# A hybrid attention and SSM block: 42 quads with seven products instead of 38, their sums and last blocks in other buffers, the scan's matmuls in program order

## The chip, the cores and the metric

The kernel runs on one core of a Trainium2 chip. The core has a matrix engine (TensorE, PE in the profile), a vector engine (VectorE, DVE), a scalar engine (ScalarE, ACT), a general engine (GpSimd, POOL) and a sync engine (SyncE, SP) that issues DMA transfers; each works through its own list of instructions in order and waits for the others by semaphores. The metric is the device time of one execution in microseconds (us), the median of several runs. Inputs and results are fp32.

## The reference, cut to what matters

One block on 256 rows of 2048: a norm, one wide projection, attention in three dilations with 16 heads, an SSM (convolution, a chunked scan in 8 groups), two gates, and an output projection. The shapes of the weights are 2048 columns wide per q, k, v, z_a, g_a, g_s, 4096 for z_s and xs, 1024 for B and C each.

```python
def hybrid_layer(x, ...):
    hn = rms_norm(x, norm_w)
    proj = hn @ w_in
    q, k, v, z_a, z_s, xbc, dt_raw, g_a, g_s = jnp.split(proj, split_points, axis=-1)
    ...
    outs, lses = ...            # dilated_window_attention for (128, 1), (512, 4), (2048, 16)
    wts = jax.nn.softmax(jnp.stack(lses), axis=0)
    o_a = jnp.einsum('pbsh,pbshe->bshe', wts, jnp.stack(outs)) * jax.nn.silu(z_a)
    xbc = jax.nn.silu(causal_depthwise_conv(xbc, conv_w, conv_b))
    xs, bm, cm = jnp.split(xbc, ...)
    y = ssd_chunked_scan(xs, dt, a, bm, cm) + d_skip * xs
    y = rms_norm(y * jax.nn.silu(z_s), ssm_norm_w)
    merged = jax.nn.sigmoid(g_a) * (o_a @ w_attn_branch) + jax.nn.sigmoid(g_s) * (y @ w_ssm_branch)
    return x + merged @ w_out   # a last rms_norm follows
```

## The kernel before

**Weights.** All weights lie in one array of units, 128 rows by 1024 columns of fp32 (512 KB). Each unit is split in two parts of a reduced format: ScalarE makes the high part h (line 265), VectorE the rest l = w - h (line 266). The left side is split likewise, and a product is the sum of three matmuls, xh.h, xh.l and xl.h (`triple`). Units come through a ring of five places in SBUF (`ring`, tag "w"), the parts through rings of four (h, l, and hl for the seven-product quads). SP issues all of these loads in one queue.

**Stages.** First come the projections that have the weights as columns (z_s, xs, B, C with the SSM's groups 1 to 7, stage by stage), then six pair stages made by `gemm_pair`: ssm (y @ w_ssm_branch, depth 4096, 16 quads), v, later ga, attn (o_a @ w_attn_branch) and out (8 quads each). Between v and ga lie the projections of q, k and z_a and the attention itself. Each pair stage runs in two halves, c = 0 and c = 2, of 1024 columns; "attn half 2" below is the stage ("attn", 2). All 256 rows and 1024 columns stand as 2 x 2 blocks of 128 x 512, four accumulators.

**Quads.** A quad is two units (256 of the depth) times the 2 x 2 blocks: eight products, 24 matmuls of 128x512. For the quads in `S_QUADS` seven products do (Winograd's form of Strassen's scheme): 21 matmuls, for which sums of blocks are needed on both sides. On the weights' side a quad has wa (its first unit), wt (two sums) and the last block, wc, which is half a unit (in the code of before the right half of wb). From them come the split parts ha, la; hc, lc; htt, ltt (of wt) and, after wa -= wt, htu, ltu. The products that are common to several accumulators gather in four more banks (pp) over the stage, and `fold` adds them once at the end.

**Sums made ahead.** Two of the additions for wt can be made ahead (`sum_jobs`): a job loads the blocks into a buffer that stands idle, VectorE subtracts twice (128x512), and the result is spilled to DRAM under the quad's name (t_ssm, t_ga, t_attn, t_out), from where the stage loads it as wt. A copy on POOL ties a job to a place in the program. A quad without such a job loads its second unit whole and makes the two subtractions in place (lines 518 and 524). Of before's 38 quads 30 have their sums ahead: 12 of 13 in ssm, all of ga, attn and out; the seven of v are made in place. Left sums (sx_y for ssm, sx_x, sx_o, sx_m) are also made early and spilled, and fetched when a unit of the stage before is reached (`fetch_left`).

**The scan.** For each of the 8 groups `scan` (line 788) issues 32 matmuls in 16 pairs: the two of a pair write the upper and the lower 64 rows of the result. `after` sets at which unit of the projections the group's scan starts.

**What sets the order.** The code is written stage by stage, but the order on each engine is the scheduler's, by priorities (`high_priority`) and its own estimate of time. It may move a matmul ahead of others that the program wrote before it, where no data forbids it. Rings free a place when the last reader of the old content is done, and a transfer on SP that waits for its place holds those behind it.

Of the kernel before, what the change touches and what calls it, by code (L numbers as in the profile page):

```python
# [15 lines left out]
P = 128  # L16
# [23 lines left out]
A_ORDERS = {0: (0, 1, 2, 4, 3, 6, 5, 7), 2: (0, 2, 1, 4, 3, 6, 5, 7)}  # L40
V_ORDERS = {0: None, 2: (0, 2, 1, 4, 3, 5, 6, 7)}
# [16 lines left out]
SUMS_SSM = [(("ssm", c), q) for c in (0, 2) for q in S_QUADS[("ssm", c)]]  # L58
SSM_EVERY, LEFT_EVERY, ATT_EVERY = 10, 11, 4
SUM_LAG = 3  # L60

# [125 lines left out]
def hybrid_block(ctx: ExitStack, tc: tile.TileContext, wall, xt, x, pk_d, cst_d, fw_d, out):  # L187
    nc = tc.nc
    ve, ac, gp, pe = nc.vector, nc.scalar, nc.gpsimd, nc.tensor

# [221 lines left out]
    def plain_unit(tag, q):  # L412
        return FIRST[tag] + 2 * max(n for n in range(q + 1) if n not in S_QUADS[tag])
# [34 lines left out]
    def gemm_pair(tag, x_of, n_kt, sxs, swap, extra={}, close=1, order=None):  # L448
# [22 lines left out]
        for at, q in enumerate(order):  # L471
# [24 lines left out]
            wa, wb = ring(f"wa{n}"), ring(f"wb{n}")  # L496
# [19 lines left out]
            with tc.high_priority(L_AHEAD):  # L516
# [5 lines left out]
                part(wb[:, 512:], hc[:, :512], lc[:, :512])  # L522
# [131 lines left out]
    with tc.tile_pool(name="ssm", bufs=2) as sp:  # L654
# [125 lines left out]
        def scan(g, state):  # L780
            xdt, gt = state["xdt"], state["gt"]
            yps = [bank("m2", 2, f"yp{g}_{v}") for v in range(2)]
            for k in (3, 2, 1, 0):
                v, i = divmod(k, 2)
                for a, b, c, o in ((0, S, 0, 0), (S, 384, 1, P)):
                    for j in range(2):
                        n, rows, col = 2 * i + j, 64 * j, i * S + o
                        pe.matmul(
                            yps[v][rows : rows + 64, col : col + b - a], xdt[:, v, c, n, :], gt[:, 4 * v + n, a:b],
                            start=(c == 0), stop=(c == 1),  # L790
                        )
# [66 lines left out]
        for c in GS_BEFORE[0]:  # L858
# [6 lines left out]
            SUMS_SSM, range(begin + 1, FIRST[("xs", 26)], SSM_EVERY),  # L865
# [10 lines left out]
        for g in range(GROUPS):  # L876
# [9 lines left out]
            for t in range(max(4 * g, 1), 4 * g + 4):  # L886
# [4 lines left out]
                if t % 4 == 3:  # L891
# [7 lines left out]
                    for q in (2 * g, 2 * g + 1):  # L899
                        if q in SX_Y:  # L900
# [34 lines left out]
    for n, q in enumerate(SX_X[:1]):  # L935
        fetch_left(sx_of_x, xk, 1, ("x", q), two_kts(XT, q), 0, FIRST[("ssm", 2)] + 24 + 4 * n)
    with tc.tile_pool(name="xp", bufs=1) as xp:
        sxs = {}

# [234 lines left out]
```

## Time and profile before

| what | us |
|---|---|
| median of 3 runs | 1389.33 (1388.9 to 1390.08) |
| the profiled execution | 1389.12 |
| its span, first to last instruction | 1387.3 |
| TensorE busy | 1376.8 |
| VectorE busy | 1148.3 |
| ScalarE busy | 828.9 |
| GpSimd busy | 130.3 |
| DMA, mean rate | 240 GB/s |

The profile's numbers are in us, where nothing else is said. "x24" counts instructions. An arrow a<-b names result and operand. An idle time stands with the engine that ended it. In the rows of stretches each engine has its busy time and, in brackets, its instructions; then come the granted clock, the DMA engines' busy share and GB/s. In the rows of the timeline the first number is the start after the span's begin, the second the duration; in the chain's rows the second is the time that the piece adds. Lines of transfers give count, KB each, and the median us from issue to landing.

### The profile page before, as it was taken

Reading aid. Unit: us, or ns where it says so; the run is one execution under the profiler, and the core shown is the slowest. Engines: PE = TensorE matmul, PEld = TensorE weight load, DVE = VectorE, ACT = ScalarE, POOL = GpSimd, SP = SyncE. Lnnn points to the kernel's source line nnn. Section 1 sums busy time; section 2 is a strip of 40 time slices with the busy share of each in tenths; the row PEclk is TensorE's granted clock in tenths of the full one; section 3 lists DMA queues with packets and bytes.
Section 4 is the critical chain, followed back from the end, with each engine's and each line's share of the span. In section 5 each row is a group of like instructions: output and inputs, shape, how many; then the busy total and the mean of one; then the engine's idle time right before and its main releaser. Section 6 shows DMA issues by size and latency. Waiting matters only on the chain.

```text
span 1387.3 us, 20558 instructions
## 1 busy us (share of the span) xinstructions
PE 1376.8 (99%) x7272; PEld 1171.5 (84%) x7272; DVE 1148.3 (83%) x1709; ACT 828.9 (60%) x1289; POOL 130.3 (9%) x201
## 2 busy tenths in 40 slices
PE   9999999999999999999999999999999999999997
PEld 7888888888888888888888888888888888888886
DVE  6898998887798888868878997777777688889897
ACT  7656677675677675765554554544544456556464
POOL 2301110010000000010000001111111000000110
PEclk9999999999999999999999999999999999999999
DMA  9766877868676866567767668888888656776764
GB/s 346 231 189 213 285 241 236 272 200 300 217 251 212 261 197 204 186 228 267 237 224 258 224 195 287 275 274 277 296 287 279 182 171 219 270 250 207 251 241 150
DMA packets 100743, 332.67 MB, mean 240 GB/s; under 512 B 11232, under 2 KB 13472, under 8 KB 100512
## 3 DMA queue, kind: packets, MB, share of 16 engines
q1 hardware_dynamic: 99920, 330.18, 72.0%
q8 instruction: 57, 0.93, 0.3%
q10 hardware_dynamic: 720, 1.18, 0.2%
q14 instruction: 46, 0.38, 0.1%
HBM read 306.87 MB, written 24.44 MB: 239 GB/s over the span
## 4 chain that ended last, share of the span: by engine, by line
PE 98%; DMA 0%; DVE 0%; POOL 0%; SPq 0%; ACT 0%; issue 0%; POOLq 0%; DVEq 0%; ACTq 0%
PE ps_zs L318 8%; PE ps_xs L318 8%; PE ps_zs L321 4%; PE ps_q L318 4%; PE ps_k L318 4%; PE ps_za L318 4%; PE ps_xs L321 4%; PE ps_ssm L463 3%; PE ps_ssm L464 3%; PE ps_ssm L465 3%; PE ps_q L321 2%; PE ps_k L321 2%; PE ps_za L321 2%; PE ps_gs L402 2%; PE ps_gs L403 2%; PE ps_gs L401 2%
## 5 line engine op out<-in xcount | busy, mean ns | idle before, releaser
L265 ACT ACTIVATE h<-w 128x1024 fp32r<-128x1024 f32 (+1 forms) x408 | 425.7, 1049 | 357.2 <-issue 82.8
L266 DVE TENSOR_TENSOR l<-w,h 128x1024 fp32r<-128x1024 f32 (+1 forms) x408 | 491.9, 1211 | 160.9 <-ACT h L265 158.5
L318 PE MATMUL ps_zs<-XT,h 128*128 128x512 f32 x496 | 175.7, 395 | 0.0
L318 PE MATMUL ps_xs<-XT,h 128*128 128x512 f32 x496 | 175.2, 394 | 0.0
L321 PE MATMUL ps_zs<-XT,l 128*128 128x256 f32 x496 | 139.6, 282 | 0.0
L321 PE MATMUL ps_xs<-XT,l 128*128 128x256 f32 x496 | 139.6, 281 | 0.0
L318 PEld LDWEIGHTS ps_xs<-XT,h 128*128 128x128 f32 x496 | 93.0, 188 | 21.3
L318 PEld LDWEIGHTS ps_zs<-XT,h 128*128 128x128 f32 x496 | 93.1, 188 | 20.9
L321 PEld LDWEIGHTS ps_zs<-XT,l 128*128 128x128 f32 x496 | 93.6, 189 | 1.9 <-issue 1.1
L321 PEld LDWEIGHTS ps_xs<-XT,l 128*128 128x128 f32 x496 | 93.6, 189 | 0.8 <-issue 0.6
L318 PE MATMUL ps_q<-XT,h 128*128 128x512 f32 x256 | 92.3, 404 | 0.0
L318 PE MATMUL ps_k<-XT,h 128*128 128x512 f32 x256 | 89.8, 394 | 0.0
L318 PE MATMUL ps_za<-XT,h 128*128 128x512 f32 x256 | 89.5, 394 | 0.0
L321 PE MATMUL ps_q<-XT,l 128*128 128x256 f32 x256 | 71.0, 277 | 0.0
L321 PE MATMUL ps_k<-XT,l 128*128 128x256 f32 x256 | 71.0, 277 | 0.0
L321 PE MATMUL ps_za<-XT,l 128*128 128x256 f32 x256 | 70.9, 277 | 0.0
L318 PEld LDWEIGHTS ps_k<-XT,h 128*128 128x128 f32 x256 | 48.0, 188 | 11.1
L318 PEld LDWEIGHTS ps_za<-XT,h 128*128 128x128 f32 x256 | 48.0, 188 | 11.0
L318 PEld LDWEIGHTS ps_q<-XT,h 128*128 128x128 f32 x256 | 48.0, 188 | 10.9
L751 ACT ACTIVATE gt<-acb,acT 128x128 f32<-128x128 f32 x128 | 43.8, 391 | 19.5 <-DMA acb<-acum_d 16.4
L512 ACT ACTIVATE ha<-wa 128x1024 fp32r<-128x1024 f32 x38 | 40.0, 1054 | 20.8 <-DMA wa<-in_wall 7.4
L513 DVE TENSOR_TENSOR ltu<-wa,htu 128x1024 fp32r<-128x1024 f32 x38 | 46.4, 1222 | 5.8 <-ACT htu L512 5.4
(633 smaller groups left out, 3270.2 us busy)
## 6 DMA issues: line engine op xcount, KB each, us to landing
w<-in_wall SPq DMA_DIRECT2D x404, 512.0 KB, 4.5
wa<-in_wall SPq DMA_DIRECT2D x38, 512.0 KB, 4.4
th_a<-in_wall SPq DMA_DIRECT2D x18, 512.0 KB, 5.5
acb<-acum_d SPq DMA_DIRECT2D x32, 256.0 KB, 3.8
wb<-in_wall SPq DMA_DIRECT2D x30, 256.0 KB, 3.7
sums_at<-in_wall SPq DMA_DIRECT2D x12, 512.0 KB, 4.0
t_ssm<-sums_at SPq DMA_DIRECT2D x12, 512.0 KB, 4.3
wt<-t_ssm SPq DMA_DIRECT2D x12, 512.0 KB, 4.9
```

The lines of the kernel that those rows point to most:

```text
L265: ac.activation(h[:, a:b], w[:, a:b], AF.Copy)
L266: ve.tensor_tensor(l[:, a:b], w[:, a:b], h[:, a:b].bitcast(F32), ALU.subtract)
L318: pe.matmul(acc, h[:, kk, :], m, start=(kt == 0), stop=False)
L321: pe.matmul(acc[:, S:], l[:, kk, :], m[:, :S], start=False, stop=(kt == KT - 1))
L401: pe.matmul(accs[i], xh, h[:, kk], start=(kt == 0), stop=False)
L402: pe.matmul(accs[i], xh, l[:, kk], start=False, stop=False)
L463: pe.matmul(acc, xh, h, start=start, stop=False)
L464: pe.matmul(acc, xh, l, start=False, stop=False)
L465: pe.matmul(acc, xl, h, start=False, stop=stop)
L512: ac.activation(h, src, AF.Copy)
L513: ve.tensor_tensor(l, src, h.bitcast(F32), ALU.subtract)
L751: ac.activation(g4[:, n, b], acb[:, j, b // 2 * P : b // 2 * P + P], AF.Relu, scale=-1.0, bias=sc[:, h : h + 1],)
```

## The change

- `S_QUADS`: seven products for ssm quad 12 in both halves, v quad 5 in half 0 and attn quad 5 in half 2; 42 in all. The orders in which quads come within a half are new for ssm, and changed for v half 0 and attn half 2.
- `SUMS_SSM` now lists ssm and v, except for ssm quad 12 (`IN_PLACE`). The jobs start at three units of each of groups 1 to 6: 18 places for 13 + 8 entries, and the zip ends with the shorter, so v half 2 quads 4, 5 and 6 have no job and are summed in place. Sums ahead: 13 ssm, 5 v, 8 ga, 7 attn, 4 out; in place: 5.
- `place` in `gemm_pair`: a quad with its sum ahead no longer takes ring places for wt and the last block (wc), but seats in a `room`, a buffer that is idle in that stage, round robin: for ssm two seats for wc in the stage's pool, for v all in room_v, for ga wt in th_a's idle half, for attn wt and wc in `fin` (a new name and buffer for the result of attn, where vt was), for out in room_o. In attn the seats of wc are `fin[:, 0, :512]` and `fin[:, 1, :512]`, which are also two of the four blocks that take the result of half 0. The count of seats runs on from one half to the next.
- The left sums of ssm quads 12 and 13 are made in the stage itself (`Y_LATE`), by way of a ring place, and not spilled and fetched.
- `scan` issues its matmuls under `in_order`, so the scheduler keeps them in the order written, with nothing between that comes from elsewhere in the list.

```diff
--- before.py
+++ after.py
-A_ORDERS = {0: (0, 1, 2, 4, 3, 6, 5, 7), 2: (0, 2, 1, 4, 3, 6, 5, 7)}
-V_ORDERS = {0: None, 2: (0, 2, 1, 4, 3, 5, 6, 7)}
+A_ORDERS = {0: (0, 1, 2, 4, 3, 6, 5, 7), 2: (0, 2, 1, 4, 3, 5, 6, 7)}
+V_ORDERS = {0: (0, 1, 2, 4, 3, 5, 6, 7), 2: (0, 2, 1, 4, 3, 5, 6, 7)}
...
 S_QUADS = {
-    ("ssm", 0): (5, 7, 8, 10, 11, 13), ("ssm", 2): (3, 5, 7, 8, 10, 11, 13),
-    ("v", 0): (2, 4, 6), ("v", 2): (2, 4, 5, 6), ("ga", 0): (2, 4, 5, 6), ("ga", 2): (2, 4, 5, 6),
-    ("attn", 0): (2, 4, 6), ("attn", 2): (2, 4, 6), ("out", 0): (3, 5), ("out", 2): (3, 5),
+    ("ssm", 0): (5, 7, 8, 10, 11, 12, 13), ("ssm", 2): (3, 5, 7, 8, 10, 11, 12, 13),
+    ("v", 0): (2, 4, 5, 6), ("v", 2): (2, 4, 5, 6), ("ga", 0): (2, 4, 5, 6), ("ga", 2): (2, 4, 5, 6),
+    ("attn", 0): (2, 4, 6), ("attn", 2): (2, 4, 5, 6), ("out", 0): (3, 5), ("out", 2): (3, 5),
 }
-SX_Y = S_QUADS[("ssm", 2)]
+Y_ORDERS = {0: (0, 1, 2, 3, 5, 4, 7, 8, 6, 10, 11, 9, 12, 14, 13, 15), 2: (0, 3, 1, 5, 2, 7, 8, 4, 10, 11, 6, 12, 9, 13, 14, 15)}
+Y_LATE = {12: 4, 13: 6}
+SX_Y = sorted({*S_QUADS[("ssm", 0)], *S_QUADS[("ssm", 2)]}, key=Y_ORDERS[0].index)
...
-SUMS_SSM = [(("ssm", c), q) for c in (0, 2) for q in S_QUADS[("ssm", c)]]
-SSM_EVERY, LEFT_EVERY, ATT_EVERY = 10, 11, 4
+IN_PLACE = {"ssm": [(0, 12), (2, 12)]}
+SUMS_SSM = [(t, q) for t in (("ssm", 0), ("ssm", 2), ("v", 0), ("v", 2)) for q in S_QUADS[t] if (t[1], q) not in IN_PLACE.get(t[0], ())]
+SUM_UNITS = 2, 9, 16
+LEFT_EVERY, ATT_EVERY = 11, 4
...
+    seats = {}
+
+    def gemm_pair(tag, x_of, n_kt, sxs, swap, extra={}, close=1, order=None, room={}):
...
+            def place(kind):
+                if not room.get(kind):
+                    t = ring(f"{kind}{n}")
+                    return t[:, 512:] if kind == "wc" else t
+                seats[kind] = seats.get(kind, -1) + 1
+                return room[kind][seats[kind] % len(room[kind])]
+
+            wa = ring(f"wa{n}")
             nc.sync.dma_start(wa, wall[n])
             if made:
-                wt = ring(f"wt{n}")
+                wt, wc = place("wt"), place("wc")
                 nc.sync.dma_start(wt, presum[tag, q])
-                nc.sync.dma_start(wb[:, 512:], wall[n + 1, :, 512:])
+                nc.sync.dma_start(wc, wall[n + 1, :, 512:])
             else:
-                wt = wb
-                nc.sync.dma_start(wb, wall[n + 1])
+                wt = ring(f"wb{n}")
+                wc = wt[:, 512:]
+                nc.sync.dma_start(wt, wall[n + 1])
...
-                part(wb[:, 512:], hc[:, :512], lc[:, :512])
+                part(wc, hc[:, :512], lc[:, :512])
...
+                        in_order(
+                            pe.matmul(
+                                yps[v][rows : rows + 64, col : col + b - a], xdt[:, v, c, n, :], gt[:, 4 * v + n, a:b],
+                                start=(c == 0), stop=(c == 1),
+                            )
...
-            SUMS_SSM, range(begin + 1, FIRST[("xs", 26)], SSM_EVERY),
+            SUMS_SSM, [FIRST[("B", g)] + n for g in range(1, 7) for n in SUM_UNITS],
...
+    def room_of(t, n_wt, n_wc):
+        t = t.rearrange("p (n m) -> p n m", m=512)
+        return {
+            "wt": [t[:, 2 * n : 2 * n + 2].rearrange("p n m -> p (n m)") for n in range(n_wt)],
+            "wc": [t[:, 2 * n_wt + n] for n in range(n_wc)],
+        }
+
     with tc.tile_pool(name="xp", bufs=1) as xp:
         sxs = {}
+        ssm_room = room_of(xp.tile([P, ROOM_SSM * 512], F32, name="room_s", tag="room"), 0, ROOM_SSM)
...
+        def left_y(q):
+            spare = Y_SPARE[q]
+            sx = new_sx(xp, sum(s == spare for s in Y_SPARE.values()), spare, f"y{q}")
+            sxs[q] = turn_x(sx, ring(f"sxt_y{q}").rearrange("p (n m) -> p n m", n=2), two_kts(yT, q), spare)
...
-                ("ssm", c), lambda kt: kt_of(yT, kt), 2 * KT, sxs, c == 2, {} if c else {2: [scale_gate]}
+                ("ssm", c), lambda kt: kt_of(yT, kt), 2 * KT, sxs, c == 2, {} if c else {2: [scale_gate], **{u: [lambda q=q: left_y(q)] for q, u in Y_LATE.items()}},
+                1, Y_ORDERS[c], ssm_room,
...
+    room = room_of(big.tile([P, 6 * 512], F32, name="room_v", tag="yo0a"), 2, 2)
...
+        room = {"wt": [th_a[:, i, UNIT:] for i in range(2)]}
...
-        fin = vt
+        fin = big.tile([P, 2, D], F32, name="fin", tag="yo1a")
+        room = {"wt": [fin[:, i, UNIT:] for i in range(2)], "wc": [fin[:, i, :512] for i in range(2)]}
...
-            dst = blocks(vt, c)
+            es, prods = gemm_pair(
+                ("attn", c), lambda kt: kt_of(oaT, kt), KT, sx_of_o, c == 2, order=A_ORDERS[c], room=room
+            )
+            dst = blocks(fin, c)
...
+        out_room = room_of(big.tile([P, 6 * 512], F32, name="room_o", tag="yo1b"), 2, 2)
```

The order before, on TensorE, around group 1's scan (yp; ps_zs and ps_xs are projections, h and l the parts of the weights). One lone matmul of yp stands 24 us ahead of the rest:

```order
L321 MATMUL ps_xs9_2151<-XT_76,l66_2182 128x256
L318 MATMUL ps_zs9_2224<-XT_76,h67_2227 128x512
L788 MATMUL yp1_1_2478<-gt1_1879,xdt1_1946 64x256
L321 MATMUL ps_zs9_2224<-XT_76,l67_2228 128x256
...
L318 MATMUL ps_zs11_2464<-XT_76,h75_2467 128x512
L788 MATMUL yp1_1_2478<-gt1_1879,xdt1_1946 64x256
L788 MATMUL yp1_1_2478<-gt1_1879,xdt1_1946 64x128 x2
...
L788 MATMUL yp1_0_2477<-gt1_1879,xdt1_1946 64x256 x2
```

The same places after:

```order
L324 MATMUL ps_zs9_2237<-XT_76,h67_2240 128x512
L327 MATMUL ps_zs9_2237<-XT_76,l67_2241 128x256
...
L324 MATMUL ps_zs11_2482<-XT_76,h75_2485 128x512
L806 MATMUL yp1_1_2491<-gt1_1888,xdt1_1955 64x256 x2
L806 MATMUL yp1_1_2491<-gt1_1888,xdt1_1955 64x128 x2
...
L806 MATMUL yp1_0_2490<-gt1_1888,xdt1_1955 64x256 x2
```

All 32 stand together at the later place, and so in all eight groups; before, groups 1, 2 and 6 were cut.

SP's queue ahead of attn half 2, whose first seven-product quad has the units 437 and 438, before:

```order
L254 DMA w434_12566<-in_wall 128x1024 [waits DMAHW6_49,DVE_49]
L497 DMA wa437_12600<-in_wall 128x1024 [waits DMAHW7_49,DVE_49]
L500 DMA wt437_12603<-t_attn2_2_10147 128x1024 [waits DMAHW0_49,DVE_49]
L501 DMA wb437_12601<-in_wall 128x512 [waits DMAHW1_49,DVE_49]
L254 DMA w435_12644<-in_wall 128x1024 [waits DMAHW2_49,DVE_49]
```

and after:

```order
L260 DMA w434_12639<-in_wall 128x1024 [waits DMAHW1_49,DVE_49]
L513 DMA wa437_12673<-in_wall 128x1024 [waits DMAHW2_49,DVE_49]
L260 DMA w435_12715<-in_wall 128x1024 [waits DMAHW3_49,DVE_49]
L260 DMA w436_12721<-in_wall 128x1024 [waits DMAHW5_49,DVE_49]
L513 DMA wa441_12751<-in_wall 128x1024 [waits DMAHW7_49,DMAHW4_49,DVE_49]
L260 DMA w439_12793<-in_wall 128x1024 [waits DMAHW0_49,DVE_49]
L517 DMA fin_12264<-in_wall 128x512 [waits DMAHW6_49,DVE_49]
```

The last block of unit 438 went from a ring place right behind wa437 to a seat in `fin`, four weight loads later, where it waits for VectorE.

VectorE there, before (ps_attn0_n are the results of attn half 0; line 1080 adds the folded products, 1071 adds th_a, 1072 makes the merged sum in th_s):

```order
L1080 TENSOR_TENSOR vt_7730<-ps_attn0_3_12192,vt_7730 128x512
L1071 SCALAR_TENSOR_TENSOR th_a_7731<-th_a_7731,vt_7730 128x512
L513 TENSOR_TENSOR la437_12607<-wa437_12600,ha437_12606 128x1024
L1072 SCALAR_TENSOR_TENSOR th_s_90<-th_a_7731,th_s_90 128x512
L513 TENSOR_TENSOR lc437_12611<-wb437_12601,hc437_12610 128x512
...
L266 TENSOR_TENSOR l435_12647<-w435_12644,h435_12646 128x1024
```

and after:

```order
L1125 TENSOR_TENSOR fin_12264<-ps_attn0_3_12268,fin_12264 128x512
L1114 SCALAR_TENSOR_TENSOR th_a_7796<-th_a_7796,fin_12264 128x512
L530 TENSOR_TENSOR la437_12678<-wa437_12673,ha437_12677 128x1024
...
L1115 SCALAR_TENSOR_TENSOR th_s_90<-th_a_7796,th_s_90 128x512
L543 TENSOR_TENSOR wa437_12673<-wa437_12673,fin_12264 128x1024
...
L530 TENSOR_TENSOR lc437_12682<-fin_12264,hc437_12681 128x512
L272 TENSOR_TENSOR l435_12718<-w435_12715,h435_12717 128x1024
```

The parts keep their place among the merges, but lc437 now reads the block from `fin`, whose load waits for the row of line 1114 above; on ScalarE hc437 stands directly ahead of h435, h436 and htu437, as it stood ahead of the former two before.

More of the change, by code (lines that the diff above doesn't have):

```diff
@@ L410, in keep_left, with plain_unit @@
         spill(lefts, key, f"sxd_{key[0]}{key[1]}", sx.bitcast(F32), [2, 4 - spare, P])
-    def plain_unit(tag, q):
-        return FIRST[tag] + 2 * max(n for n in range(q + 1) if n not in S_QUADS[tag])
+    def plain_unit(tag, at, order):
+        return FIRST[tag] + 2 * [q for q in order[: at + 1] if q not in S_QUADS[tag]][-1]
     def new_sx(pool, bufs, spare, name):
@@ L899, in hybrid_block @@
                     for q in (2 * g, 2 * g + 1):
-                        if q in SX_Y:
+                        if q in SX_Y and q not in Y_LATE:
                             after(
@@ L969, in hybrid_block @@
         for c in (0, 2):
-            es, prods = gemm_pair(("v", c), lambda kt: XT[:, kt, :], KT, sx_of_x, c == 2, order=V_ORDERS[c])
+            es, prods = gemm_pair(
+                ("v", c), lambda kt: XT[:, kt, :], KT, sx_of_x, c == 2, order=V_ORDERS[c], room=room
+            )
             dst = blocks(vt, c)
@@ L1051, in hybrid_block @@
             )
+        room = {"wt": [th_a[:, i, UNIT:] for i in range(2)]}
         for c in (0, 2):
-            es, prods = gemm_pair(("ga", c), lambda kt: XT[:, kt, :], KT, sx_of_x, c == 2, order=G_ORDERS[c])
+            es, prods = gemm_pair(
+                ("ga", c), lambda kt: XT[:, kt, :], KT, sx_of_x, c == 2, order=G_ORDERS[c], room=room
+            )
             open_gate(c, es, prods)
@@ L1074, in attend @@
         def attend(c):
-            es, prods = gemm_pair(("attn", c), lambda kt: kt_of(oaT, kt), KT, sx_of_o, c == 2, order=A_ORDERS[c])
-            dst = blocks(vt, c)
+            es, prods = gemm_pair(
+                ("attn", c), lambda kt: kt_of(oaT, kt), KT, sx_of_o, c == 2, order=A_ORDERS[c], room=room
+            )
+            dst = blocks(fin, c)
             with tc.high_priority(M_AHEAD) if c else nullcontext():
```

18 lines of the change are left out of this document (9 added, 9 removed).

## Prediction

> **What bounds the kernel now.** I read the page's engine table first, then its chain, then the list of waits, then equal stretches of time, and only then single places.
>
> ```profile
> PE 1376.8 (99%) x7272; PEld 1171.5 (84%) x7272; DVE 1148.3 (83%) x1709; ACT 828.9 (60%) x1289; POOL 130.3 (9%) x201
> PE 98%; DMA 0%; DVE 0%; POOL 0%; SPq 0%; ACT 0%; issue 0%; POOLq 0%; DVEq 0%; ACTq 0%
> ```
>
> TensorE (PE) is busy for 99% of the span of 1387.3 us and makes up 98% of the chain that ended last. A modelled end can hide small gaps, so the list of TensorE's waits comes next, and after it the stages, one row each: both ssm halves, attn halves 0 and 2, and out half 0.
>
> ```profile
> PE warm L592 <- DVE ssq L589: 1.4, 1, 1.4
> PE ps_first L366 <- ACT h L265: 0.7, 1, 0.7
> ```
>
> ```profile
> 584.70:667.90 83.20, 83.20 (x373) 69.02 (x372) 63.68 (x69) 47.82 (x52) 8.06 (x8) 1.00 0.76 255
> 667.90:750.90 83.00, 83.00 (x368) 68.76 (x367) 66.55 (x66) 45.81 (x49) 2.42 (x2) 1.00 0.70 231
> 1207.60:1249.20 41.60, 41.60 (x186) 34.43 (x185) 36.58 (x41) 25.56 (x30) 0.00 (x0) 1.00 0.70 230
> 1249.20:1292.40 43.20, 43.20 (x200) 35.77 (x199) 41.25 (x53) 23.63 (x30) 1.43 (x1) 1.00 0.70 227
> 1292.40:1336.30 43.90, 43.90 (x203) 36.38 (x202) 37.16 (x47) 22.91 (x29) 7.26 (x4) 1.00 0.76 265
> ```
>
> TensorE waits twice in the whole run, for 2.1 us. In each stage it is full at the granted clock of 1.00, and VectorE (DVE, third busy number) is below it: closest in attn half 2, 41.25 of 43.20. So a matmul that goes is worth its time, as long as VectorE, ScalarE and the loads keep ahead.
>
> **Term 1: four more seven-product quads.** One plain quad is 24 matmuls of 128x512, a seven-product one 21. Attn half 0 holds five and three of them, 183 matmuls in the 41.60 us of its row: 0.227 us each. Single rows agree:
>
> ```profile
> 1248.72 0.39 PE L464 MATMUL ps_attn<-l,oaTb 128*128 128x512 f32 x1
> 1248.95 0.39 PE L465 MATMUL ps_attn<-h,oaTb 128*128 128x512 f32 x1
> 1249.18 0.39 PE L463 MATMUL ps_attn<-h,oaTa 128*128 128x512 f32 x1
> 1249.40 0.39 PE L464 MATMUL ps_attn<-l,oaTa 128*128 128x512 f32 x1
> ```
>
> Starts are 0.227 apart though one lasts 0.39: matmuls overlap, and the pitch counts. 4 x 3 x 0.227 = **-2.72 us**.
>
> Here a page speaks against the reading. The Trainium skill, "Trainium Kernel Development and Optimization", Best Practices, has it that the busy share of matmuls is a poor gauge, since they are pipelined, and that the busy share of weight loads is a good one; the engine table gives 84% for them, which would leave TensorE room, and by 12 loads at the 0.188 us of this profile the term would be an estimated -2.26. The equal starts decide for the pitch.
>
> **Term 2: the scan held together.** The scan's 32 matmuls run as pairs, two halves of 64 columns side by side. The chain shows what a group takes whole and what in pieces (the counts are those on the chain):
>
> ```profile
> 164.51 2.75 PE yp L788 x32
> 202.07 0.58 PE yp L788 x2
> 226.01 2.75 PE yp L788 x23
> 261.03 0.80 PE yp L788 x6
> 287.43 2.31 PE yp L788 x20
> 368.86 2.75 PE yp L788 x32
> 524.34 0.58 PE yp L788 x2
> 550.96 2.75 PE yp L788 x23
> ```
>
> Groups 1 and 6 lose one half of a pair to a place 24 us earlier; the lone half takes 0.58, and the rest still 2.75, since the partner runs alone. Group 2 is cut after three matmuls: 0.80 + 2.31. Against 2.75 the surplus is 0.58 + 0.36 + 0.58 = 1.52. Entering such a place delays the next matmul a little more:
>
> ```profile
> 201.68 0.40 PE L318 MATMUL ps_zs<-XT,h 128*128 128x512 f32 x1
> 202.00 0.65 PE L788 MATMUL yp<-gt,xdt 128*64 128x256 f32 x2
> 202.58 0.39 PE L321 MATMUL ps_zs<-XT,l 128*128 128x256 f32 x1
> ```
>
> Between the two ps_zs lie 0.90 where 0.227 is the pitch: 0.67 lost, 0.09 over the 0.58. With 0.08 to 0.09 for each of the three cuts the term is **-1.77** (ends: -1.52 without it and -1.79). The kept order puts each group whole at the later place, where its operands were already there.
>
> **VectorE, at nothing.** A quad with its sum made ahead costs VectorE four tensor operations of 128x1024 and one of 128x512; a plain quad two of the former; a quad in place two more of 128x512.
>
> ```profile
> 1245.63 1.23 DVE L513 TENSOR_TENSOR ltt<-wt,htt 128x1024 fp32r<-128x1024 f32 x1 [1.48 <-ACT htt L512]
> 1246.77 1.22 DVE L266 TENSOR_TENSOR l<-w,h 128x1024 fp32r<-128x1024 f32 x1
> 1247.91 1.28 DVE L1080 TENSOR_TENSOR vt<-ps_attn,vt 128x512 f32<-128x512 f32 x2
> 1249.10 0.68 DVE L1071 SCALAR_TENSOR_TENSOR th_a<-th_a,vt 128x512 f32<-128x512 f32 x1
> 1249.70 0.69 DVE L1080 TENSOR_TENSOR vt<-ps_attn,vt 128x512 f32<-128x512 f32 x1
> ```
>
> Pitches are 1.14 and 0.60, so 5.16, 2.28 and 6.36. Two of the new quads have their sum ahead (v and attn: 2 x 2.88), two are in place (ssm quad 12 in both halves: 2 x 4.08): +13.9. Five v quads and one ssm quad are no longer in place: 6 x 1.20 = -7.2. Seven more sums made ahead: 7 x 1.20 = +8.4. Some 5 more for the left sums of ssm quad 12, an estimate from operations of these two sizes: +20 on 1148.3, spread over 750 us, against 239 us in which VectorE idles. By stage: ssm half 2 goes from 66.55 by 4.08 - 1.20 to 69.4 of 82.3; attn half 2 with out half 0 gains 2.9 on 78.4 of 87.1. TensorE covers that. If the cover went, each microsecond over would be one of loss; the thin place is attn half 2, taken below.
>
> **Sums ahead, at nothing.** v is not made whole: 13 ssm and 8 v jobs meet 18 places (6 groups by 3), and the last three, of v's second half, stay in place. Seven more jobs bring POOL's copies, two loads and a spill each.
>
> ```profile
> q1 hardware_dynamic: 99920, 330.18, 72.0%
> wt<-t_attn SPq DMA_DIRECT2D x6, 512.0 KB, 4.7
> wb<-in_wall SPq DMA_DIRECT2D x30, 256.0 KB, 3.7
> ```
>
> About 7.5 MB more on 330 at 72% is 1.6 points; POOL stands at 9%. Both lie beside TensorE. A load in a room frees ring places on SP's queue, so weights behind it come no later, except where it waits for the room itself.
>
> **The new wait: start of attn half 2.** Before, the last block of unit 437 lay in the ring long before the stage began (its ring load, 256 KB, takes 3.7), and ScalarE made its high part early:
>
> ```profile
> 1249.66 0.61 ACT L512 ACTIVATE hc<-wb 128x512 fp32r<-128x512 f32 x1
> 1252.11 0.68 DVE L1071 SCALAR_TENSOR_TENSOR th_a<-th_a,vt 128x512 f32<-128x512 f32 x1
> 1252.10 1.07 ACT L265 ACTIVATE h<-w 128x1024 fp32r<-128x1024 f32 x1 [1.82 <-PE ps_attn L465]
> ```
>
> ```profile
> 1257.30 0.66 PE mtp L1064 x6
> ```
>
> Now its seat is the second one in `fin`, which holds block 2 of attn half 0 until VectorE has added it to th_a. Call the stage's first matmul T (1249.18). If VectorE comes as before, that addition is ninth from 1247.91: it ends at 1247.91 + 8 x 0.60 + 0.68 = T+4.2. If only the last matmul of half 0 limits it (1248.95 + 0.39), one eviction and one addition later it ends near T+1.5. The load lands 3.7 later, T+5.2 to T+7.9; hc takes 0.61 (T+5.8 to T+8.5), and behind it in ScalarE's queue stand h435, h436 and htu437, on VectorE lc437, l435, l436: h435 is done near T+6.9 to T+9.6. In the order 27 matmuls and ten transposes (0.11 each) stand ahead of hc437: 27 x 0.227 + 1.1 = T+7.2, and h435 is due a matmul later, T+7.4. The wait is **0 to +2.2**. VectorE's 1.48 us of idling at 1244 says that it isn't far behind there; I take **+1.0**.
>
> The Trainium skill, "DMA: Bandwidth & Descriptors", Anatomy of one DMA, puts a transfer at about 2.0 us plus bytes over 436 GB/s, measured on another path; for this load that is an estimated 2.6, which would take 1.1 us off the wait's upper end. The row here says 3.7 and stands.
>
> **Sum.** -2.72 - 1.77 + 1.0 = -3.5. The profiled execution took 1389.12 (span 1387.3), the median of three is 1389.33, 0.21 above; on the median that is **1385.8 us**.
>
> **Rivals.** (a) *The wait takes most of the gain.* The attn wait at 2.2, a few tenths at each of a handful of other stage starts: +2.7 to +4, 1387.5 to 1389. For: the chain load, ScalarE, VectorE above. Against: VectorE idle at 1244.
> (b) *TensorE has room as by the weight loads' 84%, or the scan, held together, waits for its last operand as long as it saves.* Then only part comes: 1387 to 1389. Against: the two short waits.
> (c) *Slower.* The 15 seven-product quads of ssm share two seats of 512 columns. A load that waits for its seat holds SP's queue, and the weights behind it come late. ScalarE does wait for such blocks now:
>
> ```profile
>   DMA wb<-in_wall: 29.9, 20
> ```
>
> That is 20 waits of 1.5 us, none of which reaches TensorE. It decides from (4.49 + 2.78) / 15 = 0.48 us on TensorE per quad; at 0.7 each it is +10.5 - 4.5, 1395. Against: a seat comes round after two such quads, 2 x 21 x 0.227 = 9.5 us, while load, hc and lc take 3.7 + 0.6 + 0.7 = 5.0.
> (d) *The change does less than its words* in v: three sums in place, 3 x 1.20 us on VectorE, hidden as before; no time.
>
> **How the numbers follow.** 0.2% (2.78 us) is about what a measurement here tells from no change. The forecast with a wait of 0 to 1.7 (1384.8 to 1386.5): 0.58. Rivals (a) and (b), within 0.2%: 0.25 and 0.08. Rival (c): 0.09. So faster 0.58, same 0.33, slower 0.09. The range runs from 1384.3 (no wait, less the half microsecond by which runs differ) to 1389.2, the upper end of (a) and (b); some 0.13 is left out.
>
> **What would show it.** Right: 12 matmuls of 128x512 fewer; yp as x32 of 2.75 in all eight groups; at the start of attn half 2 a TensorE wait for ACT hc or h of about a microsecond, with ScalarE waiting for a load into fin just before; no wait in ssm, v and out; VectorE some 20 us busier. Wrong: waits of TensorE on ps_ssm or ps_v behind room loads (c), a stretch of idle ahead of yp (b), or an attn wait over 2 us (a).

## The result, and the profile after

The changed kernel takes 1385.80 us, the median of 9 runs (1384.94 to 1386.88), against 1389.97 us (1388.90 to 1390.43) for the kernel before in 9 runs: a ratio of 0.9971, 95% interval 0.9963 to 0.9980. It is faster by 4.2 us, where 3.5 was forecast. That the time forecast, 1385.8, was met to the tenth is partly luck: the forecast stood on a median of three runs, 1389.33, which with more runs rose by 0.64. What has to be explained is a gain of 4.2, and which of the terms made it.

The head of the page of the changed kernel, and the list of TensorE's waits (us in total, times, longest):

```profile
span 1383.1 us, 20652 instructions
PE 1373.2 (99%) x7260; PEld 1169.1 (85%) x7260; DVE 1164.5 (84%) x1742; ACT 834.2 (60%) x1300; POOL 138.6 (10%) x222
q1 hardware_dynamic: 103824, 341.46, 72.2%
```

```profile
PE warm L609 <- DVE ssq L606: 1.4, 1, 1.4
PE ps_first L372 <- ACT h L271: 0.2, 1, 0.2
```

TensorE has 12 matmuls fewer, VectorE 16 us more work (20 were estimated), the queue 11 MB more (7.5 were estimated). TensorE waits at the same two places at the start as before, and at no new one: not at attn half 2. The profiled execution took 1384.94, the lowest of the nine, and its span is 4.2 under before's 1387.3.

The chain's rows of the scan in the changed kernel, start and duration:

```profile
164.43 2.75 PE yp L806 x32
224.64 2.75 PE yp L806 x32
285.43 2.75 PE yp L806 x32
367.59 2.75 PE yp L806 x32
428.39 2.75 PE yp L806 x32
489.01 2.75 PE yp L806 x32
549.63 2.75 PE yp L806 x32
580.69 2.75 PE yp L806 x32
```

All eight groups are whole. (The profile has two records for each of these fp32 matmuls: x32 are the 16 matmuls, or 8 pairs, of a group, and the x2 of before was one matmul. The "32 matmuls in 16 pairs" of the text before the result are records.) From the first scan to the last, before took 582.01 - 164.51 = 417.50 and the changed kernel 580.69 - 164.43 = 416.26: 1.24 less, where the scan alone should give 1.77.

The later stages, by rows of single groups; the two numbers ahead of the semicolon are the first and the last start. Before:

```profile
L463 PE MATMUL ps_v<-h,XT x72: 389/389/389, 751.0 to 834.3; 128*128 128x512 f32 x72
L463 PE MATMUL ps_ga<-h,XT x64: 389/389/577, 1124.1 to 1207.0; 128*128 128x512 f32 x64
L463 PE MATMUL ps_attn<-h,oaTa x48: 389/389/477, 1207.7 to 1276.7; 128*128 128x512 f32 x48
L463 PE MATMUL ps_out<-h,mT x96: 389/389/474, 1292.5 to 1378.1; 128*128 128x512 f32 x96
```

After:

```profile
L471 PE MATMUL ps_v<-h,XT x64: 389/389/389, 748.3 to 832.0; 128*128 128x512 f32 x64
L471 PE MATMUL ps_ga<-h,XT x64: 389/389/577, 1120.8 to 1203.7; 128*128 128x512 f32 x64
L471 PE MATMUL ps_attn<-h,oaTa x48: 389/389/397, 1204.4 to 1273.3; 128*128 128x512 f32 x48
L471 PE MATMUL ps_out<-h,mT x96: 389/389/478, 1283.5 to 1374.0; 128*128 128x512 f32 x96
```

The changed kernel is ahead by 1.3 at the last scan, 2.7 when v begins (two more seven-product quads in ssm), 3.3 at ga and still at attn (one in v), and 4.1 at out's last h (one in attn). Each quad's step is, to 0.1, the 0.68 that three matmuls take. So the four quads give their -2.72 in full; the rest, -1.3, was made before the ssm stage. Of it the scan's -1.77 is the forecast's term, and -0.37 comes at the very start (before and after differ in the first 50 us, where TensorE waits for its first h: 0.7 and 0.2); what is left over is something that costs +0.8.

That something is the pitch of the projections. Between interruptions they run as pairs of a 512- and a 256-column matmul. The same place, right after the small matmuls cbp ahead of group 3's scan, in the timeline of before:

```profile
352.87 0.39 PE L318 MATMUL ps_xs<-XT,h 128*128 128x512 f32 x1
353.22 0.39 PE L318 MATMUL ps_xs<-XT,h 128*128 128x512 f32 x1
353.56 0.39 PE L318 MATMUL ps_xs<-XT,h 128*128 128x512 f32 x1
353.91 0.39 PE L318 MATMUL ps_xs<-XT,h 128*128 128x512 f32 x1
```

and after:

```profile
351.30 0.40 PE L324 MATMUL ps_xs<-XT,h 128*128 128x512 f32 x1
351.66 0.40 PE L324 MATMUL ps_xs<-XT,h 128*128 128x512 f32 x1
352.00 0.40 PE L324 MATMUL ps_xs<-XT,h 128*128 128x512 f32 x1
352.36 0.40 PE L324 MATMUL ps_xs<-XT,h 128*128 128x512 f32 x1
```

Three pairs take 1.04 us there and 1.06 here. Over the whole stretch of 16 us the mean pitch is 346 ns a pair before and 353 after, at the same granted clock of 1.00, with nothing waiting. As long as the two widths strictly alternate, the mean pitch is one of two values, 346.7 or 353.3: every such run of 11 pairs or more between 45 and 585 us has one of the two, to 0.2, in these two traces and in four of the experiments. A stretch with a mean between them, such as 350, holds a run of each, and changes over where two matmuls of one width stand in a row. Which one a run gets differs between the two kernels in ten or so places: ahead of the scans of groups 0, 2, 3, 4 and 5 the changed kernel has 353 for 346, at group 1 it is the other way round.

### The profile page after: what moved, and what is told of

Read it like the earlier page. It is cut to its first block, busy times and chain, and to the rows that moved or that the text cites. A ratio compares the mean times of both kernels' runs of the same rounds, so it can differ in the third digit from the quotient of the medians.

```text
span 1383.1 us, 20652 instructions
## 1 busy us (share of the span) xinstructions
PE 1373.2 (99%) x7260; PEld 1169.1 (85%) x7260; DVE 1164.5 (84%) x1742; ACT 834.2 (60%) x1300; POOL 138.6 (10%) x222
## 4 chain that ended last, share of the span: by engine, by line
PE 98%; DMA 0%; DVE 0%; POOL 0%; SPq 0%; ACT 0%; issue 0%; POOLq 0%; DVEq 0%; ACTq 0%
PE ps_zs L324 8%; PE ps_xs L324 8%; PE ps_zs L327 4%; PE ps_k L324 4%; PE ps_q L324 4%; PE ps_za L324 4%; PE ps_xs L327 4%; PE ps_ssm L471 3%; PE ps_ssm L472 3%; PE ps_ssm L473 3%; PE ps_q L327 2%; PE ps_k L327 2%; PE ps_za L327 2%; PE ps_gs L409 2%; PE ps_gs L407 2%; PE ps_gs L408 2%
## 5 line engine op out<-in xcount | busy, mean ns | idle before, releaser
L271 ACT ACTIVATE h<-w 128x1024 fp32r<-128x1024 f32 (+1 forms) x400 | 416.0, 1048 | 330.9 <-issue 79.6
L272 DVE TENSOR_TENSOR l<-w,h 128x1024 fp32r<-128x1024 f32 (+1 forms) x400 | 482.1, 1212 | 128.8 <-ACT h L271 126.5
L529 ACT ACTIVATE ha<-wa 128x1024 fp32r<-128x1024 f32 x42 | 44.3, 1055 | 35.7 <-PE ps_ssm L473 9.1
L530 DVE TENSOR_TENSOR ltu<-wa,htu 128x1024 fp32r<-128x1024 f32 x42 | 51.3, 1223 | 12.7 <-ACT htu L529 12.5
L530 DVE TENSOR_TENSOR la<-wa,ha 128x1024 fp32r<-128x1024 f32 x42 | 51.3, 1222 | 10.8 <-ACT ha L529 10.6
L529 ACT ACTIVATE htu<-wa 128x1024 fp32r<-128x1024 f32 x42 | 44.3, 1054 | 24.2 <-PE ps_ssm L473 7.2
```

What stands on the lines that cost most here:

```text
L271: ac.activation(h[:, a:b], w[:, a:b], AF.Copy)
L272: ve.tensor_tensor(l[:, a:b], w[:, a:b], h[:, a:b].bitcast(F32), ALU.subtract)
L529: ac.activation(h, src, AF.Copy)
L530: ve.tensor_tensor(l, src, h.bitcast(F32), ALU.subtract)
```

## The experiments

Times are medians, beside the kernel before on the same chip. "Drift" is the start of a matmul less the start of the same matmul in the profiled execution of the changed kernel.

### The scan alone, and the change without it

`e1_scan_only` is the kernel before with the scan's kept order:

```diff
-                        pe.matmul(
-                            yps[v][rows : rows + 64, col : col + b - a], xdt[:, v, c, n, :], gt[:, 4 * v + n, a:b],
-                            start=(c == 0), stop=(c == 1),
-                        )
+                        tc.keep_in_program_order(
+                            pe.matmul(
+                                yps[v][rows : rows + 64, col : col + b - a], xdt[:, v, c, n, :], gt[:, 4 * v + n, a:b],
+                                start=(c == 0), stop=(c == 1),
+                            )
+                        )
```

> The kernel before with one edit: the scan's matmuls kept in program order. Theory (a lone half costs as much as a pair, and each place of the scan costs 0.09 us to enter): all eight groups take 2.75 us whole, 1.77 us less on TensorE, so about 1388.2 against 1390.0, at most 0.9 us off that because the pitch of the projections' matmuls shifts by a few ns. Rival (the held scan waits for its last operand as long as it saves): 1390.0, with a TensorE wait ahead of yp.

`e2_no_order` is the changed kernel without it:

```diff
-    in_order = tc.keep_in_program_order
+    in_order = lambda inst: inst
```

> The changed kernel without the scan's kept order. The scheduler then cuts six groups: in five one whole pair goes ahead alone, in one (group 5) three matmuls do. Theory (only a lone half loses time; a whole pair moved costs the entry alone): 5 x 0.09 + 0.44 = 0.9 us more than the changed kernel, 1386.7. Rival (every cut costs some 0.6 us, whatever is cut off): 3.6 us more, 1389.4, which is the time before, and the kept order would then be most of the gain.

The kernel before with the scan held takes 1387.81 (11 runs) against 1390.27, ratio 0.9986 (0.9977 to 0.9994). Its chain has all groups whole:

```profile
164.46 2.75 PE yp L789 x32
580.14 2.75 PE yp L789 x32
```

From first to last scan that is 415.68, 1.82 less than before's 417.50: the term of -1.77 is right, by itself, and no wait stands ahead of yp. The changed kernel, whose groups are just as whole, takes 416.26, 0.58 longer: this part of the +0.8 is seen directly, and another 0.29 lies in the stretch ahead of group 0's scan. (In this execution 0.6 us were lost again at attn half 2, with a short wait for VectorE's l.)

Without the kept order the changed kernel takes 1385.68 (5 runs), no more than with it, though six groups are cut. The rows of two groups:

```profile
402.46 0.58 PE yp L806 x4
428.66 2.32 PE yp L806 x28
462.99 0.79 PE yp L806 x6
489.39 2.31 PE yp L806 x20
```

A pair that goes ahead alone takes 0.58, as the lone half did before, and the rest 2.32: 2.90 against 2.75, so 0.15 for such a cut; three matmuls ahead (x6) cost 0.79 + 2.31 - 2.75 = 0.35. By these rows halves lose time and moved pairs little: 5 x 0.15 + 0.35 = 1.1 on these rows, 0.9 forecast, not 3.6. But the time is not 0.9 longer. The drift at the last scan is -0.26, of which -0.13 comes from the start: between the scans the pitch gave the 1.1 back. In the changed kernel, then, holding the scan buys nothing that can be measured; against the kernel before, whose cuts went through pairs, it buys 1.8.

### The changed kernel once more

`e4_again` has no edit.

> The changed kernel once more, unedited, for its trace. Against the kernel before, its projections ran at a pitch of 353 ns per pair of matmuls (512 and 256 columns) in four stretches of about 17 us ahead of a scan where before had 347, +0.85 us in all up to the ssm stage. Theory (the pitch in a stretch belongs to the program, set by what interrupted the stretch before it): the same stretches are slow again, to within 0.1 us. Rival (it belongs to the single execution): other stretches are slow, and the sum differs by more than 0.3 us.

1386.24 (6 runs; with the first nine the median of 15 is 1385.9). The scans of this execution:

```profile
165.21 2.75 PE yp L806 x32
...
581.47 2.75 PE yp L806 x32
```

Each is 0.78 later than in the first execution, 416.26 from the first to the last as there. Between 50 and 800 us the drift is 0.779 in every stretch of 20 us, to a nanosecond: the pitch belongs to the program, and the rival falls. What differs between executions is the start (TensorE waits 2.0 us for its first h here, 0.2 there, and is 0.78 later behind it), a step of 0.34 at the start of q, and, in other executions than this one, a load at the end of the kernel, which a later section comes to.

### C and B one or two projections later

The edit moves four small matmuls per group and nothing else:

```diff
-DT_LAG, CB_LAG, TURN_LAG, GT_LAG, Y_LAG, S_LAG, M_LAG = 2, 5, 3, 2, 11, 2, 2
+DT_LAG, CB_LAG, TURN_LAG, GT_LAG, Y_LAG, S_LAG, M_LAG = 2, 6, 3, 2, 11, 2, 2
```

> The changed kernel with each group's four small matmuls of C and B one projection later; the same work. Theory (the pitch of the projections falls into one of a few fixed values, 346 or 353 ns per pair, after each interruption, by how TensorE comes out of it): a different set of stretches is slow, and the drift against the changed kernel up to the ssm stage is 0.3 us or more either way, with no wait of TensorE. Rival (the pitch hangs on what the stretch itself is, not on what came before): the same stretches are slow, drift under 0.1 us.

> The kernel with C and B one projection later, once more, for more timed runs and a second trace. Theory (the pitch belongs to the program, the wait at the first room load of out to the execution): drift against the changed kernel -1.10 us between 50 and 583 us again, to within 0.05; the step near 1314 anywhere from 0 to 1.2 us; the median 0.5 to 1.5 us under the changed kernel's 1385.8 to 1386.2. Rival (the first 1384.7 was a lucky few runs): drift elsewhere, median 1385.6 or above.

> The changed kernel with the four small matmuls of C and B two projections later. Theory (the pitch after an interruption is one of a few values and is set by where TensorE is interrupted): again another set of slow stretches than in the changed kernel and than with one projection later, a drift of up to 2 us either way up to the ssm stage, no waits. Rival (later is better by itself): a drift of -1.1 us or lower, as with one projection later.

One later: 1384.66 (4 runs) and, again, 1384.77 (5 runs; ratios 0.9958, interval 0.9946 to 0.9971, and 0.9965, 0.9952 to 0.9979). The scans of the second:

```profile
164.57 2.75 PE yp L806 x32
579.73 2.75 PE yp L806 x32
```

415.16 from first to last, 1.10 less than the changed kernel's 416.26, and the drift between 50 and 583 us falls by 1.10 in both executions, by the same steps, most of them 0.2. Other stretches are slow, the work is the same, and up to there no wait of TensorE is added or gone. Two later: 1385.40 (5 runs), and the drift falls by 0.73 by other steps. So the rival that later is better by itself falls. One later is the fastest version that was run; over nine runs its median, 1384.77, is 1.2 under the 15 of the changed kernel. The intervals of the two versions' ratios overlap, so the times alone don't separate them; the drift of 1.10 in two traces does.

### The new seat in attn

`e3_late_seat` moves the seats to the blocks that are merged last:

```diff
-        room = {"wt": [fin[:, i, UNIT:] for i in range(2)], "wc": [fin[:, i, :512] for i in range(2)]}
+        room = {"wt": [fin[:, i, UNIT:] for i in range(2)], "wc": [fin[:, i, 512:UNIT] for i in range(2)]}
```

> The changed kernel with attn's seats for the last block moved by 512 columns, to the blocks that VectorE adds to th_a last (the addition ends 1.7 us later). Theory (the new wait exists, but had 0.8 us in hand on ScalarE's h435): the load of unit 438's last block starts near T+4.2, lands near T+6.7, hc and h435 end near T+7.3 and T+8.3, h435 is due at T+7.4: TensorE waits 0.7 to 1.0 us there and the time is 1386.6 to 1386.8. Rival (the place has far more room than the order shows): no TensorE wait, 1385.8.

In the changed kernel the chain of the forecast is there. ScalarE, VectorE and TensorE at the start of attn half 2 (T is 1245.84 in this trace):

```profile
1250.90 0.63 ACT L529 ACTIVATE hc<-fin 128x512 fp32r<-128x512 f32 x1 [4.47 <-DMA fin<-in_wall]
1251.44 1.99 ACT L271 ACTIVATE h<-w 128x1024 fp32r<-128x1024 f32 x2
...
1247.64 0.69 DVE L1114 SCALAR_TENSOR_TENSOR th_a<-th_a,fin 128x512 f32<-128x512 f32 x1
...
1253.00 0.48 PE L471 MATMUL ps_attn<-hc,sx_o 128*128 128x512 f32 x1
```

ScalarE does stand 4.47 us for the load into `fin`. But the addition that frees the seat ends at 1248.33, T+2.5, between the two ends that were given (1.5 and 4.2), and the load is used 2.57 later, not 3.7 (in seven traces with this seat it lands 2.4 to 2.6 after its issue): hc ends at T+5.7 and is due at T+7.2, h435 ends near T+6.7 and is due at T+7.4. Some 0.7 to 1.5 us are in hand, and TensorE does not wait.

With the later seat the time is 1386.68 (12 runs), and TensorE waits:

```profile
1253.85 0.63 ACT L529 ACTIVATE hc<-fin 128x512 fp32r<-128x512 f32 x1 [0.76 <-PE mtp L1107]
1254.53 0.50 PE L471 MATMUL ps_attn<-hc,sx_o 128*128 128x512 f32 x1 [0.20 <-ACT hc L529]
```

The drift rises from 0.19 ahead of this place to 0.91 behind it: 0.72 us, in the band of 0.7 to 1.0; the row above counts 0.20 of it as a wait. So the mechanism is real: a later load into `fin` makes TensorE late. But the way there was not the expected one. The seat came free 1.7 later, as intended; the load then landed 3.46 after its issue (1250.28 to 1253.74, just ahead of hc, though the row names mtp), where about 2.5 was expected; and the edit changed the order too, with htu ahead of hc on ScalarE and six more transposes (mtp) ahead of hc on TensorE, which made hc due later. So the margin of the changed kernel is used up by 1.7 and 1.0 together; that a seat 1.7 later would cost by itself was not shown.

### 38, 43 quads

`e5_quads38` takes the four quads back, and leaves the rest; `e6_quads43` adds one more:

```diff
-    ("ssm", 0): (5, 7, 8, 10, 11, 12, 13), ("ssm", 2): (3, 5, 7, 8, 10, 11, 12, 13),
-    ("v", 0): (2, 4, 5, 6), ("v", 2): (2, 4, 5, 6), ("ga", 0): (2, 4, 5, 6), ("ga", 2): (2, 4, 5, 6),
-    ("attn", 0): (2, 4, 6), ("attn", 2): (2, 4, 5, 6), ("out", 0): (3, 5), ("out", 2): (3, 5),
+    ("ssm", 0): (5, 7, 8, 10, 11, 13), ("ssm", 2): (3, 5, 7, 8, 10, 11, 13),
+    ("v", 0): (2, 4, 6), ("v", 2): (2, 4, 5, 6), ("ga", 0): (2, 4, 5, 6), ("ga", 2): (2, 4, 5, 6),
+    ("attn", 0): (2, 4, 6), ("attn", 2): (2, 4, 6), ("out", 0): (3, 5), ("out", 2): (3, 5),
...
-Y_LATE = {12: 4, 13: 6}
+Y_LATE = {13: 6}
```

> The changed kernel with before's 38 seven-product quads (ssm quad 12 plain in both halves, v quad 5 of half 0, attn quad 5 of half 2); rooms, orders, sums ahead and the held scan stay. Theory (12 matmuls at 0.227 us, all on the path): 2.7 us more than the changed kernel, 1388.6. Rival (the gain of the change comes from the rooms and the orders, TensorE had room for the matmuls): less than 1 us more, under 1387.

```diff
-A_ORDERS = {0: (0, 1, 2, 4, 3, 6, 5, 7), 2: (0, 2, 1, 4, 3, 5, 6, 7)}
+A_ORDERS = {0: (0, 1, 2, 4, 3, 5, 6, 7), 2: (0, 2, 1, 4, 3, 5, 6, 7)}
...
-    ("attn", 0): (2, 4, 6), ("attn", 2): (2, 4, 5, 6), ("out", 0): (3, 5), ("out", 2): (3, 5),
+    ("attn", 0): (2, 4, 5, 6), ("attn", 2): (2, 4, 5, 6), ("out", 0): (3, 5), ("out", 2): (3, 5),
```

> The changed kernel with a 43rd seven-product quad (attn quad 5 of half 0, its sum made ahead). Theory (the path is TensorE's and VectorE still has room there, 2.9 us more in a stage where it idles 5): 0.68 us less, 1385.2. Rival (VectorE or the seats become late at the end of attn half 0): a TensorE wait there of 0.5 us or more, 1385.8 or above.

With 38 the time is 1389.40 (11 runs), the ratio to before 0.9997 (0.9988 to 1.0005): all that is left of the change is not to be told from nothing, and the version with the quads is 3.5 faster, where 2.7 was expected. Four of its drift's steps are 0.64 to 0.68, at the places of the four quads, so the matmuls are worth 2.7 of it; 1.2 us more came in out half 0, with a wait (below).

With 43 the time is 1391.51 (12 runs), the ratio 1.0005. The quad is not worth 0.68; by the median it costs 5.6. The times stand in two groups, five from 1388.6 to 1389.6 and seven from 1391.4 to 1393.5, and the traced run is the slowest of all, 1393.49. TensorE's waits, and the rows behind them:

```profile
PE ps_out L471 <- ACT h L271: 2.4, 1, 2.4
PE ps_attn L471 <- ACT htu L529: 1.2, 1, 1.2
PE ps_attn L471 <- ACT hc L529: 1.1, 1, 1.1
```

```profile
1251.32 0.63 ACT L529 ACTIVATE hc<-fin 128x512 fp32r<-128x512 f32 x1 [4.17 <-DMA fin<-in_wall]
...
1263.28 0.63 ACT L529 ACTIVATE hc<-fin 128x512 fp32r<-128x512 f32 x1 [6.22 <-DMA fin<-in_wall]
...
1316.77 8.72 POOL L624 COPY fw<-h 128x1 f32<-128x1 f32 x1 [13.79 <-ACT h L271]
```

So the forecast's cover, sums of VectorE's work under TensorE's by stage, isn't enough to admit a quad. TensorE loses nothing in attn half 0, where the quad was added, but 3.1 us in half 2, around htu and at hc, and ScalarE stands for a load into `fin` ahead of each: with a fourth quad in half 0 the round of the seats begins half 2 at the other seat. The other 4.2 us of this trace have another cause, which need not be the quad's. A copy of one column on POOL, 0.2 us in the changed kernel, took 8.7 here, and SP's queue stood for it, 15.2 us against 6.5 (its load of the final norm's weights, fw, is tied to that copy); the weights behind it came late, TensorE waited 2.4 us, and then ran eight matmuls 0.43 apart instead of 0.227, with a granted clock of 0.66 in the mean from 1335 to 1340. Whether this is what parts the two groups of times was not shown.

### The rooms

`e7_no_room` sends every sum and last block through the ring:

```diff
-                if not room.get(kind):
+                if True:
```

> The changed kernel with every sum and last block back in the ring of five places, the rest as it is. Theory (the rooms only take pressure off the ring, which had slack): TensorE waits a few tenths in all, 1385.8 to 1386.5. Rival (42 quads need the rooms: the ring then holds weight loads back): several waits of TensorE on h or hc, 1388 or more.

1393.27 (11 runs), ratio 1.0025 (1.0015 to 1.0035), slower than before. The drift rises by 4.7 in ssm, between 600 and 700 us, by 0.4 at q and ga and by 1.4 in attn and out. TensorE's waits in ssm, and ScalarE's there:

```profile
PE ps_ssm L471 <- ACT h L271: 1.1, 1, 1.1
PE pp_ssm L471 <- ACT htu L529: 0.6, 1, 0.6
```

```profile
616.55 0.63 ACT L529 ACTIVATE hc<-wc 128x512 fp32r<-128x512 f32 x1 [4.66 <-DMA wc<-in_wall]
```

Loads come late. A seven-product quad takes three of the ring's five places, as before, but there are two more of them in ssm, in other orders, and two left sums pass through the ring too; which of these weighs most was not separated. The four quads need the rooms: with the rest of the change and 38 quads nothing is won, with 42 quads and no rooms 3.6 us are lost, with both 4.2 are won.

### Out's first room load, and all sums of v

`e9_cb6_out` has C and B one later and half 0 of out in the ring; `e10_v_all` is the changed kernel with 24 places for its sums:

```diff
-                2 if c0 else 1, O_ORDERS[c0], out_room,
+                2 if c0 else 1, O_ORDERS[c0], out_room if c0 else {},
```

> The kernel with C and B one projection later, and half 0 of out back in the ring, whose rooms lie in th_a's place and can be loaded only when th_a is free, 7.9 us before their first use in the changed kernel's trace. Theory (that load ends within tenths of its use, and TensorE waits 0 to 1.2 us there from one execution to the next): no wait and no step at 1314, 0.3 to 0.8 us less than with C and B later alone, about 1384.0. Rival (the ring has no place to spare there either): 1384.7 or above, with a wait on another load.

```diff
-SUM_UNITS = 2, 9, 16
+SUM_UNITS = 2, 7, 12, 17
```

> The changed kernel with 24 places for its sums in groups 1 to 6 (2, 7, 12, 17 for 2, 9, 16), so that all eight sums of v are made ahead. Theory (3.6 us less on VectorE in v half 2, 3.6 more before, both beside TensorE): no change beyond the pitch, 1385.0 to 1386.8. Rival (the eighth sum removes the 0.34 us that TensorE loses in some executions at the start of q): 0.3 less.

The rooms of out lie in th_a's place. In the changed kernel the loads are issued when th_a has been read, and the first of them is used 8 us later:

```profile
1302.59 0.33 SPq L516 DMA_DIRECT2D room_o<-t_out  x1
...
1310.56 1.06 ACT L529 ACTIVATE htt<-room_o 128x1024 fp32r<-128x1024 f32 x1 [2.63 <-DMA room_o<-t_out]
```

In that execution it was in time; with C and B later (the first execution) it was 1.2 us later against the same work, htu waited, and 0.85 us were lost at one step (0.57 in `e3_late_seat`, 0.58 in `e11_cb7`, 1.2 in `e5_quads38`, 0 in the second execution with C and B later). With half 0 in the ring that wait is gone, but another takes its place:

```profile
PE ps_out L473 <- DVE mT L281: 0.4, 1, 0.4
```

```profile
1308.10 2.48 DVE L281 TENSOR_TENSOR mT<-mtp,mT 128x512 fp32r<-128x512 f32 x4
```

The drift rises by 0.65 there and the time is 1386.65 (11 runs), 1.9 above the same kernel with its room. So the time came out as the rival has it, but not by its cause: the wait is for VectorE, not for a load. With the loads early in the ring, VectorE makes ltt, lc and the subtraction of the first quad ahead of mT, and mT starts at 1308.10, where it starts at 1305.53 in `e12_cb6_again`. The trace, of the fastest of the 11 runs, accounts for 0.65 of the 1.9; the rest stays open.

With all eight sums of v made ahead the time is 1388.57 (10 runs), 2.7 above the changed kernel, where none was expected. The drift shows 0.8 by pitch up to ssm, nothing in v, and 2.1 in out half 0, whose first room load goes out behind one more weight load and is used 9.6 us later:

```profile
1305.28 0.33 SPq L516 DMA_DIRECT2D room_o<-t_out  x1
...
1314.87 1.06 ACT L529 ACTIVATE htt<-room_o 128x1024 fp32r<-128x1024 f32 x1 [5.44 <-DMA room_o<-t_out]
```

So the sums that the change leaves in place cost nothing in v. Why three more jobs some 700 us earlier alter the order of loads in out was not followed; the order is the scheduler's.

## Why the prediction was right, and where not

- **TensorE bounds the kernel, and the pitch counts.** Right. Four quads gave four steps of about 0.68, seen in the stages' starts and again, backwards, with 38 quads. The estimate by weight loads, 3 x 0.188 = 0.56 a quad, is refuted by these steps.
- **The scan, -1.77.** Right by itself (-1.82 in the kernel before). In the changed kernel it stands, but what the scheduler makes without the kept order is as fast.
- **The wait at attn half 2, +1.0.** This term was mis-sized: it measured 0, and the wait for hc or h that was to show the forecast right did not appear. Its band began at 0, and the chain of merge, load, hc and h is as described; what was too long was the load (2.57 measured from release to use, against the 3.7 of the median row). With 3.7 in its place h435 would by these rows have come some 0.3 us late, an estimate. The seven traces with this seat have about 2.5, and the later seat's load took 3.46; why they differ was not shown. The Trainium skill, "DMA: Bandwidth & Descriptors", Anatomy of one DMA, gives an estimated 2.6 for this load, by a fit for another path. The 2.57 agrees with it, the 3.46 does not. The first room loads of out took 8 and 9.6 us from issue to use, with four loads issued together.
- **What took its place.** The pitch of the projections, +0.8, which the forecast had no term for; and -0.37 at the start, which changes from execution to execution. -2.72 - 1.77 + 0.82 - 0.37 = -4.04, against -4.07 between the last matmuls of the two traces. (+0.82 is what the other terms leave over up to the ssm stage; the comparison with the held scan alone shows 0.87.) The sum -3.5 was 0.7 short of the medians' -4.2. It was that near by luck: the +1.0 that did not come and the +0.8 that was not thought of nearly cancel.
- **VectorE, at nothing.** Right (+16 us for +20, no wait in any stage). The sum has a slip: of before's eight quads in place five, not six, are no longer so, which makes it +21. The way to it was too coarse: 43 quads pass the same sum, and TensorE then waits behind loads into seats.
- **The rooms, at nothing.** No cost was seen in ssm and v, and rival (c), SP held back by seats, did not come: no wait on ps_ssm. But they were not nothing: without them the time is 7.4 longer. The forecast left out what the 42 quads would have cost without rooms, and said only that no weight would come later.
- **Out's rooms.** The forecast had no term for the load that waits for th_a. It is in time in some executions and costs 0.6 to 1.2 in others.

## What to carry to other kernels

When one engine is full, a removed instruction is worth its pitch, and can be checked stage by stage from the first and last start of a group of instructions. A wait that a new dependency may bring is a chain of release, load and two conversions; take the load's time from a load in the same state of the queue, and try the chain with its release moved, which tells the margin if the order stays the same. A median of runs in two groups is not the price of one cause; look where the traced run stands among them. And where gains are of the order of 0.1%, moving an interruption by one step can be worth as much as a quad or two.

## What was not expected of the hardware

- The pitch of a run of alternating 512- and 256-column matmuls is one of two fixed values (346.7 or 353.3 ns a pair, 2% apart), kept until other matmuls, or two of one width in a row, break the alternation, at a granted clock of 1.00 and with no wait. The choice belongs to the program: two executions of one kernel agree to a nanosecond from 50 to 800 us, while two programs with the same order around a place differ. Moving four small matmuls per group by one projection was worth 1.1 us. What chooses the value stays open: in the two traces at the cbp ahead of group 3's scan, the order and the interruption's own 0.57 us are alike, and the second pair already differs.
- One half of a column pair alone takes 0.58, and so does a whole pair alone. A whole pair ahead of its group costs 0.15, a lone half 0.58.
- TensorE's wait for its first h varies by execution from 0.2 to 2.0 us, and the matmuls behind it start up to 1.1 us apart (drift -0.13 to 0.95 in the eleven other traces of the changed kernel and its variants): less than timed runs of one kernel differ (1384.9 to 1387.6 for the changed one), so it is a part of that difference and not all.
- In one trace (`e6_quads43`) the granted clock fell to 0.50 for 3.4 us, 1.5 us after a wait of TensorE of 2.4 us, and eight matmuls of 512 columns started 0.43 apart instead of 0.227.
